# Second feed-forward of the last layer: opening weights one column sooner, seven opening tiles, kept first half, inputs of the way back made beside the last tile

## The chip, the cores and the metric

The kernel runs on one core of one Trainium2 chip. The metric is the device time of one execution in microseconds (us), as the median of several runs. The core has five engines that work through their own instruction lists in order: TensorE (PE, matrix products), VectorE (DVE), ScalarE (ACT), GpSimd (POOL) and SyncE (SP, which here issues nearly all transfers).

## The reference

A diffusion backbone with `DEPTH = 2` layers on a latent stream of 1024 positions of width 1024 and a context of 256 positions. All is float32. Each layer mixes tokens in three ways, projects, adds with a gate, and then runs a gated feed-forward. Only the end of the last layer matters for this change:

```
x = x + g1 * einsum('blm,md->bld', mix, w_out[l])
h = modulate(rms_norm(x, norm2_g[l]), sh2, sc2)
g, u = split(einsum('bld,df->blf', h, w_ffn_in[l]))      # 1024 -> 2 x 2816
x = x + g2 * einsum('blf,fd->bld', silu(g) * u, w_ffn_out[l])   # 2816 -> 1024
```

In the last layer the context is no longer needed, so this tail runs on the 1024 latent positions alone.

## The kernel before

Values are held transposed: features on the 128 partitions, positions along the row. The 1024 positions are two halves of 512 (0 and 1), the width is 8 groups of 128 features (`KD = 8`), the hidden width 22 tiles of 128 (`NF = 22`). Each float32 matrix product is made of matmuls of 128x128 by 128x512 on operands that are split into a rounded upper part `hi` and a rest `lo`: hi*hi + hi*lo + lo*hi, three matmuls for each group of 128 inputs. The split of weights or values costs a cast (the `hi`) and a subtraction (the `lo`); mostly ScalarE casts and VectorE subtracts.

The tail of the last layer has four stages, one behind the other on TensorE.

*The last out-projection* (`out_proj`, L1143): for each half, eight output columns `d`, each of 24 matmuls. For each column VectorE adds the gated product to `x` (a SCALAR_TENSOR_TENSOR), ScalarE squares it and VectorE sums the squares; the new `x` is stored to the memory `XD` (`park`), to be read again at the end. The weights come from a `Stream` (L1966): raw tiles of 128x1024 loaded by SP some columns ahead, cast by ScalarE, lower half by VectorE. In column `d == KD - 3` of the second half `soon()` is called, which starts the stream of the next stage.

*The opening* (`fast_open`, L1375; first loop of `ffn_fast`, L1379). The feed-forward's first product uses a scheme of Strassen's kind: with the two halves of positions and of inputs and the gate and up weights as a 2 by 2 block product, seven products of 12 matmuls serve instead of eight: A11·B11, S2·T2, S1·T1, A12·B21, S3·T3, A22·T4 and S4·B22, 84 matmuls for each of 22 hidden tiles. A11·B11 and A12·B21 need only the first half of the positions. So the first `FIRST = 6` tiles get these two products (24 matmuls a tile) while the second half is still being normed. Their results, `kept`, stay on chip. The weights of the opening are cast and negated by ScalarE, and the lower half is made by an accumulating DMA that POOL issues (`lo=("d",)`).

Meanwhile `fast_norm1` (L1315) norms the second half and makes the operands B22, T1 to T4 out of both halves, in four turns `k` of two feature groups each (`k` and `k + 4`). A turn has, among others, four scalings (`scaled`, L1341: `x` times a column factor times the row's `1/rms`), two for half 1 and two for half 0. Half 0's scalings were made once already, in `norm_h` (L554) for `fast_norm0`. The turns are a generator (`lane`) that is stepped between the products, so that its instructions lie between the evacuations of the opening on VectorE and ScalarE. Between them a clock model (`Clock`, with `due`) decides how many steps come in at `self.adv()`. `self.finish("norm1")` issues whatever is left of it.

*The main loop* (second loop of `ffn_fast`): 22 tiles of five or seven products. A generator `prep` casts and subtracts each operand of the weights up to `AHEAD = 7` products before it is used, in tiles from the pool `big` (23 buffers). The gated hidden values are stored to `HD` in memory: for each tile one store for each half of the positions.

*The way back* (`ffn_back`, L1539): for each half and each of 8 output columns, 66 matmuls (22 hidden tiles of three). Before its first column it reads half 0's 22 hidden tiles from `HD` (`fetch`), splits each one, 20 of them into the pool `part`, two into `big`, and loads `x` from `XD` and the weights `w_ffn_out` in three groups a column (8, 8 and 6 tiles). Half 1's tiles are fetched inside the last two columns of half 0.

Instructions are issued by a helper, so that most carry L166 (or L278 for matmuls) and are known by their tiles: `big`, `half` and `part` are pools of on-chip tiles, `bank` is PSUM, where the products land, `mod` and `db` are columns of factors, `rn` the row norms.

## Time and profile before

| | |
|---|---|
| median of 3 runs | 3127.68 us (3113.27 to 3129.17) |
| the profiled execution | 3125.03 us, its span 3123.2 us |
| TensorE busy | 2887.5 us, 92% of the span, 14308 matmuls |
| VectorE busy | 1917.5 us, 61% |
| ScalarE busy | 1174.0 us, 38% |
| GpSimd busy | 684.9 us, 22% |
| mean granted TensorE clock | 0.957 of 2.4 GHz |

In the views, `x12` behind a row is the number of like instructions that are shown as one; a bracket says how long the engine stood idle before and what ended it. A timeline has the start in us from the span's beginning, then the busy time of the group. A granted clock of 0.50 is 1.2 GHz and 1.00 is 2.4 GHz; a value between is a mix of both in that stretch.

### The profile page before, as it was taken

The numbers are of one execution on the slowest core, as the hardware profiler recorded it, in microseconds if no ns is written. First come the engines' busy times: TensorE is split into PE (matmuls) and PEld (weight loads), VectorE is DVE, ScalarE is ACT, GpSimd is POOL, SyncE is SP. The second block draws the span as 40 slices with busy tenths as digits, with TensorE's granted clock in tenths as the row PEclk, the third lists the DMA queues.
The fourth block names the chain that finished last, engine by engine and source line by source line (L and its number), as shares of the span: only waits on it lengthen the run. The fifth ranks groups of instructions, "written<-read, shape, count | busy, mean of one in ns | idle before, by whom it ended". The sixth has DMA issues, their size and how long they took to land.

```text
span 3123.2 us, 38190 instructions
## 1 busy us (share of the span) xinstructions
PE 2887.5 (92%) x14308; PEld 2375.1 (76%) x14308; DVE 1917.5 (61%) x2983; ACT 1174.0 (38%) x2021; POOL 684.9 (22%) x699
## 2 busy tenths in 40 slices
PE   7799878988799999999999889999988899996999
PEld 3687767866688888888888768878866688885887
DVE  5777778967845454444333488769935866665241
ACT  4554367733422222221222235457725322223131
POOL 0100047810223232232333000038800000000000
PEclk9899979999899999999999989999989899998999
DMA  6565642265222222221110225662255332224463
GB/s 217 139 152 137 203 133 77 89 231 202 93 80 69 75 81 81 73 81 44 41 37 32 95 69 123 170 208 71 79 172 145 108 98 81 81 68 145 126 204 94
DMA packets 205288, 351.70 MB, mean 113 GB/s; under 512 B 17072, under 2 KB 103728, under 8 KB 205104
## 3 DMA queue, kind: packets, MB, share of 16 engines
q1 hardware_dynamic: 197904, 327.24, 32.9%
q0 software_dynamic: 7200, 22.02, 4.1%
q8 instruction: 113, 1.85, 0.2%
q14 instruction: 71, 0.58, 0.1%
HBM read 284.18 MB, written 65.01 MB: 112 GB/s over the span
## 4 chain that ended last, share of the span: by engine, by line
PE 69%; DVE 14%; DMA 6%; ACT 5%; issue 5%; POOL 1%; SPq 0%; ACTq 0%; DVEq 0%; POOLq 0%
PE bank L278 64%; DVE st L166 4%; DVE half L166 4%; DVE big L166 3%; PE S L278 2%; DMA half<-in_w_mod 2%; PE bank L283 2%; DVE at L166 1%; ACT half L166 1%; ACT big L166 1%; ACT p L166 1%; POOL p L166 1%; DVE part L166 1%; DMA big<-XD 1%; DMA part<-in_w_mod 1%
## 5 line engine op out<-in xcount | busy, mean ns | idle before, releaser
L278 PE MATMUL bank<-part,big 128*128 128x512 f32 (+1 forms) x7656 | 1676.3, 376 | 104.6 <-ACT big L166 49.1
L278 PEld LDWEIGHTS bank<-part,big 128*128 128x128 f32 x7656 | 1345.1, 192 | 386.5 <-ACT big L166 52.7
L166 ACT CAST big<-big 128x1024 fp32r<-128x1024 f32 (+3 forms) x316 | 270.5, 866 | 193.1 <-DMA big<-in_w_ffn_out 139.0
L278 PE MATMUL bank<-half,big 128*128 128x512 f32 (+1 forms) x1584 | 325.9, 363 | 16.4 <-DVE big L166 7.2
L278 PEld LDWEIGHTS bank<-half,big 128*128 128x128 f32 x1584 | 264.6, 192 | 72.8 <-ACT half L166 13.7
L278 PE MATMUL bank<-big,big 128*128 128x512 f32 x1152 | 303.0, 402 | 6.0 <-ACT big L166 4.0
L166 DVE TENSOR_TENSOR big<-big,bank 128x512 f32<-128x512 f32 (+1 forms) x92 | 58.7, 677 | 401.8 <-PE bank L278 233.6
L166 DVE SCALAR_TENSOR_TENSOR big<-bank,mod,big 128x512 f32<-128x512 f32 (+1 forms) x384 | 266.2, 731 | 50.9 <-PE bank L278 33.2
L166 POOL TENSOR_TENSOR big<-big,big 128x1024 fp32r<-128x1024 f32 x71 | 175.3, 2480 | 454.6 <-ACT big L166 354.7
L166 DVE TENSOR_TENSOR big<-big,big 128x512 fp32r<-128x512 f32 (+6 forms) x243 | 212.6, 884 | 90.0 <-ACT big L166 88.3
L278 PEld LDWEIGHTS bank<-big,big 128*128 128x128 f32 x1152 | 220.3, 193 | 60.6 <-ACT big L166 5.3
L166 ACT ACTIVATE half<-bank,mod 128x256 f32<-128x256 f32 x160 | 75.9, 475 | 426.3 <-PE bank L278 406.0
L166 POOL TENSOR_TENSOR p<-p,p 128x512 f32<-128x512 f32 (+1 forms) x200 | 221.6, 1108 | 16.7
L166 DVE TENSOR_REDUCE st<-S 128x1 f32<-128x1280 f32 (+1 forms) x144 | 196.0, 1362 | 12.7 <-PE S L278 12.7
L166 POOL TENSOR_TENSOR big<-big,half 128x256 f32<-128x256 f32 x160 | 122.5, 765 | 352.2 <-ACT half L166 352.2
L166 ACT ACTIVATE p<-S,st 128x1280 f32<-128x1280 f32 (+1 forms) x144 | 177.7, 1234 | 45.8 <-DVE st L166 43.1
L166 POOL TENSOR_SCALAR p<-p,st 128x512 f32<-128x512 f32 (+1 forms) x200 | 123.6, 618 | 246.3 <-DVE st L166 189.4
L278 PE MATMUL S<-kv,big 128*128 128x512 f32 (+1 forms) x672 | 162.3, 379 | 9.0 <-ACT p L166 8.5
L166 DVE TENSOR_TENSOR half<-half,bank 128x512 f32<-128x512 f32 (+1 forms) x164 | 104.6, 649 | 104.5 <-PE bank L278 103.7
L166 ACT CAST big<-half 128x512 fp32r<-128x512 f32 (+1 forms) x129 | 75.4, 599 | 219.7 <-DVE half L166 169.4
L278 PEld LDWEIGHTS S<-kv,big 128*128 128x128 f32 x672 | 123.8, 197 | 36.8 <-ACT p L166 14.2
L166 DVE SCALAR_TENSOR_TENSOR big<-big,dww,big 128x1009 f32<-128x1009 f32 (+14 forms) x120 | 148.8, 1272 | 0.4
(123 smaller groups left out, 2759.3 us busy)
## 6 DMA issues: line engine op xcount, KB each, us to landing
big<-in_w_ffn_in SPq DMA_DIRECT2D x94, 512.0 KB, 3.5
big<-in_w_ffn_out SPq DMA_DIRECT2D x54, 512.0 KB, 6.0
big<-in_w_mod SPq DMA_DIRECT2D x48, 512.0 KB, 3.7
big<-in_w_out SPq DMA_DIRECT2D x40, 512.0 KB, 5.0
half<-in_w_mod SPq DMA_DIRECT2D x64, 256.0 KB, 5.6
big<-QS SPq DMA_DIRECT2D x128, 128.0 KB, 5.1
big<-in_w_in SPq DMA_DIRECT2D x28, 512.0 KB, 4.6
HD<-half SPq DMA_DIRECT2D x44, 256.0 KB, 2.0
```

Of the source, the lines that this page charges most:

```text
L166: r = fn(*a, **k)
L278: self.tc.nc.tensor.matmul(out, lhsT, rhs, start=start, stop=stop)
L283: self.tc.nc.tensor.transpose(out, in_, ident)
```

## The change

There are three parts.

*The opening.* `soon()` of the out-projections that park their output is called one column sooner (`KD - 4`), and the opening's stream then loads three raw tiles and splits two of them there (`ahead(3, 2)` for `ahead(2, 1)`). `FIRST` is 7: a seventh tile makes its A11·B11 and A12·B21 in the opening and not in the main loop. The first weights of the main loop (`load(2)`) are asked for ahead of `finish("norm1")`.

*The norm.* `norm_h` with `keep` writes the scaled values of half 0 over `x` (which is parked in `XD` already), and `fast_norm1` reads them there: eight SCALAR_TENSOR_TENSOR go. The mixed values of half 0 and the block `blk` are dropped earlier.

*The way back's inputs.* A generator `fast_end` is stepped at the last tile's products (its first step comes at tile 20). It reads half 0's hidden tiles 0 to 19 from `HD` two at a time (512 KB each) into `big`, splits them, and loads and splits the way back's first three weight groups. Tiles 20 and 21 of half 0 are split from the chip, and not stored. Each operand of the last products (`B11`, `T2`, ...) is dropped as soon as its last product is issued, so that its buffers come free. `ffn_back` gets the finished tiles and the weight stream.

```
-FIRST = 6
+FIRST = 7
...
-                t = self.half()[:, :w]
+                t = xs[k] if keep else self.half()[:, :w]
                 nc.vector.scalar_tensor_tensor(t, xs[k], a[:, k:k + 1], rs, ALU.mult, ALU.mult)
...
-                if soon is not None and b == n - 1 and d == KD - 3:
+                if soon is not None and b == n - 1 and d == KD - (4 if park is not None else 3):
                     soon()
...
-            t12 = scaled(k, 1, rs1)
-            t11 = scaled(k, 0, rs0)
-            nc.vector.tensor_tensor(t11, t12, t11, ALU.subtract)
+            t12, t11 = scaled(k), self.half()
+            nc.vector.tensor_tensor(t11, t12, xs[k][0], ALU.subtract)
...
-            t21 = scaled(m, 0, rs0)
-            nc.vector.scalar_tensor_tensor(t21, t21, b[:, m:m + 1], t11, ALU.add, ALU.subtract)
+            t21 = self.half()
+            nc.vector.scalar_tensor_tensor(t21, xs[m][0], b[:, m:m + 1], t11, ALU.add, ALU.subtract)
...
+        load(2)
+        self.finish("norm1")
...
+        hid, back = [{}, {}], []
+        end = self.fast_end(l, ops, hid, back)
         for f in range(NF):
             whole = f >= FIRST
+            step = lambda: next(end, None) if f == NF - 1 else None
+            if f == NF - 2:
+                next(end)
...
-            store.append((f, 0, u3))
+            if f < NF - 2:
+                store.append((f, 0, u3))
+            else:
+                hid[0][f] = self.pair()
+                self.split(*hid[0][f], u3)
...
+    def fast_end(self, l, ops, hid, back):
+
+        nc = self.nc
+        raws = []
+
+        def load(f):
+            t = self.big((2, 512))
+            nc.sync.dma_start(t, self.HD[f:f + 2, :, 0:512].rearrange("f p c -> p f c"))
+            raws.append((f, t))
+
+        def split(n):
+            for _ in range(n):
+                f, t = raws.pop(0)
+                for j in range(2):
+                    hid[0][f + j] = self.pair("part")
+                    self.split(*hid[0][f + j], t[:, j, :])
+
+        st = self.fast_out(l)
+        back.append(st)
+        st.load_to(1)
+        load(0)
+        load(2)
+        yield
+
+        del ops["B11"]
+        split(2)
+        load(4)
+        load(6)
+        yield
+
+        del ops["T2"]
+        st.split_to(1)
+        split(1)
+        load(8)
+        yield
+
+        del ops["T1"]
+        st.load_to(2)
+        split(1)
+        load(10)
+        yield
+
+        del ops["B21"]
+        split(2)
+        st.split_to(2)
+        st.load_to(3)
+        load(12)
+        yield
+
+        del ops["T3"]
+        split(1)
+        load(14)
+        yield
+
+        del ops["T4"]
+        split(1)
+        st.split_to(3)
+        load(16)
+        load(18)
+        yield
+
+        del ops["B22"]
+        split(2)
...
-        for f in range(NF):
-            fetch(0, f, "part" if f < 20 else None)
...
-                plan[0].ahead(2, 1)
+                plan[0].ahead(3, 2)
```

How this stands in the engines' lists is shown at three places. First ScalarE at the end of the last out-projection, from the cast of column 5's weights on (`part` with `mod` is half 0's norm, `half<-big` the square of a finished column). The list before:

```order
L166 CAST big_20013<-big_19913 128x1024
L166 ACTIVATE part_19819<-half_20042,mod_10680 128x512
L166 ACTIVATE half_20047<-big_19666 128x512
L166 CAST big_20051<-big_19967 128x1024
L166 CAST big_20057<-big_20055 128x1024
L166 ACTIVATE big_20058<-big_20057 128x1024
L166 ACTIVATE part_19820<-half_20086,mod_10680 128x512
L166 ACTIVATE half_20094<-big_19704 128x512
L166 CAST big_20098<-big_20011 128x1024
```

and of the changed kernel at the same place, where column 5's cast is `big_20008`:

```order
L166 CAST big_20008<-big_19913 128x1024
L166 CAST big_20014<-big_20012 128x1024
L166 ACTIVATE big_20015<-big_20014 128x1024
L166 CAST big_20021<-big_20019 128x1024
L166 ACTIVATE big_20022<-big_20021 128x1024
L166 ACTIVATE part_19819<-big_19704,mod_10680 128x512
L166 ACTIVATE half_20057<-big_19666 128x512
L166 CAST big_20061<-big_19964 128x1024
L166 ACTIVATE half_20091<-big_19704 128x512
L166 CAST big_20095<-big_20006 128x1024
```

`big_20014` and `big_20021` are tiles 0 and 1 of the opening, each a cast and a negation (ACTIVATE). Four such operations now stand between the casts of two neighbouring out-projection columns (`big_20008` and `big_20061`). Before, tile 0's two (`big_20057`, `big_20058`) stood behind the corresponding cast, `big_20051`.

Second, VectorE in the second turn of the second half's norm (`half<-big,mod,half` scales, `big<-big,bank` evacuates a product of the opening). Before:

```order
L166 SCALAR_TENSOR_TENSOR half_20347<-big_19535,mod_9879,half_20238 128x512
L166 SCALAR_TENSOR_TENSOR half_20349<-big_19535,mod_9879,half_19928 128x512
L166 TENSOR_TENSOR half_20349<-half_20347,half_20349 128x512
L166 TENSOR_TENSOR big_20279<-big_20279,bank_20343 128x512
L166 SCALAR_TENSOR_TENSOR half_20371<-big_19704,mod_9879,half_20238 128x512
L166 SCALAR_TENSOR_TENSOR half_20347<-half_20347,db_20240,half_20371 128x512
L166 TENSOR_TENSOR part_20353<-half_20349,part_20352 128x512
L166 SCALAR_TENSOR_TENSOR half_20349<-half_20371,mod_10680,half_20349 128x512
L166 SCALAR_TENSOR_TENSOR part_20374<-half_20371,mod_10680,part_20373 128x512
L166 TENSOR_TENSOR part_20378<-half_20347,part_20377 128x512
L166 SCALAR_TENSOR_TENSOR half_20407<-big_19704,mod_9879,half_19928 128x512
L166 SCALAR_TENSOR_TENSOR half_20407<-half_20407,mod_10680,half_20349 128x512
```

and now:

```order
L166 SCALAR_TENSOR_TENSOR half_20369<-big_19535,mod_9879,half_20257 128x512
L166 TENSOR_TENSOR half_20371<-half_20369,big_19535 128x512
L166 SCALAR_TENSOR_TENSOR half_20384<-big_19704,mod_9879,half_20257 128x512
L166 SCALAR_TENSOR_TENSOR half_20369<-half_20369,db_20259,half_20384 128x512
L166 TENSOR_TENSOR part_20374<-half_20371,part_20373 128x512
L166 TENSOR_TENSOR big_20307<-big_20307,bank_20377 128x512
L166 SCALAR_TENSOR_TENSOR half_20371<-half_20384,mod_10680,half_20371 128x512
L166 SCALAR_TENSOR_TENSOR part_20387<-half_20384,mod_10680,part_20386 128x512
L166 TENSOR_TENSOR part_20391<-half_20369,part_20390 128x512
L166 SCALAR_TENSOR_TENSOR half_20430<-big_19704,mod_10680,half_20371 128x512
L166 TENSOR_TENSOR part_20415<-half_20371,part_20414 128x512
```

The scalings of `big_19535` and `big_19704` by half 0's norm (`half_19928`) are gone; the subtraction and the sum read `big_19535` and `big_19704` themselves.

Third, SP's list at the end of the main loop, before:

```order
L166 DMA half_23565<-HD 128x512
L166 DMA half_23570<-HD 128x512
L166 DMA half_23575<-XD 128x512
L166 DMA big_23578<-in_w_ffn_out 128x8x128
L166 DMA big_23584<-in_w_ffn_out 128x8x128
L166 DMA big_23586<-in_w_ffn_out 128x6x128
L166 DMA big_23588<-in_w_ffn_out 128x8x128
L166 DMA big_23590<-in_w_ffn_out 128x8x128
L166 DMA big_23592<-in_w_ffn_out 128x6x128
```

and now:

```order
L166 DMA HD<-half_23199 128x512
L166 DMA big_23406<-in_w_ffn_out 128x8x128
L166 DMA big_23416<-HD 128x2x512
L166 DMA big_23453<-in_w_ffn_out 128x6x128
L166 DMA big_23455<-HD 128x2x512
L166 DMA big_23482<-HD 128x2x512
L166 DMA big_23514<-HD 128x2x512
L166 DMA big_23516<-HD 128x2x512
L166 DMA HD<-half_23361 128x512
L166 DMA half_23551<-XD 128x512
L166 DMA big_23554<-in_w_ffn_out 128x8x128
L166 DMA big_23556<-in_w_ffn_out 128x8x128
```

Before, the last of 22 reads from `HD` stand ahead of the first weights `w_ffn_out`, and all of them behind the last stores. Now the reads (`128x2x512`, two tiles each) and the first weight groups lie between the stores of tiles 20 and 21 (`HD<-half_23361` is the last store), and the load of `x` and the second column's weights behind it.

## Rows read from the trace of the kernel before

**Rows 1.** The page: the span, TensorE's busy time, share and instructions, and the shares of the engines in the chain of work that ended last.

```profile
span 3123.2 us, 38190 instructions
...
PE 2887.5 (92%) x14308; PEld 2375.1 (76%) x14308; DVE 1917.5 (61%) x2983; ACT 1174.0 (38%) x2021; POOL 684.9 (22%) x699
...
PE 69%; DVE 14%; DMA 6%; ACT 5%; issue 5%; POOL 1%; SPq 0%; ACTq 0%; DVEq 0%; POOLq 0%
```

**Rows 2.** What TensorE waited for: first in 2375 to 2465, then from 2440 to the end. The columns are the total in us, the number of waits and the longest.

```profile
PE bank L278 <- ACT big L166: 14.6, 1, 14.6
PE bank L278 <- DMA big<-in_w_ffn_in: 9.8, 2, 8.8
...
PE bank L278 <- ACT big L166: 39.4, 2, 24.8
```

**Rows 3.** Stretches of the span: length, busy us of each engine (instructions), the granted clock, the DMA share and rate.

```profile
2325.00:2330.00 5.00, 5.00 (x12) 3.88 (x13) 1.14 (x2) 1.05 (x2) 0.00 (x0) 0.50 0.41 158
...
2440.00:2460.00 20.00, 10.57 (x37) 8.40 (x38) 16.70 (x26) 7.33 (x12) 0.00 (x0) 0.65 0.14 53
...
2500.00:2600.00 100.00, 100.00 (x433) 81.03 (x432) 68.75 (x108) 27.41 (x48) 0.00 (x0) 1.00 0.30 95
...
2860.00:2870.00 10.00, 0.00 (x0) 0.00 (x0) 9.23 (x15) 7.90 (x14) 0.00 (x0) 0.50 1.08 370
2870.00:2880.00 10.00, 8.38 (x25) 6.25 (x26) 5.93 (x6) 5.85 (x6) 0.00 (x0) 0.65 1.17 310
```

**Rows 4.** TensorE's timeline at an earlier short wait.

```profile
2323.47 0.74 PE L278 MATMUL bank<-big,big 128*128 128x512 f32 x2 [2.24 <-ACT big L166]
2324.73 2.08 PE L278 MATMUL bank<-big,big 128*128 128x512 f32 x4 [0.52 <-DVE big L166]
2326.61 2.76 PE L278 MATMUL bank<-part,big 128*128 128x512 f32 x6
```

**Rows 5.** SP's timeline (the issue of transfers) at the end of the out-projection.

```profile
2366.18 0.38 SPq L166 DMA_DIRECT2D big<-in_w_out  x1
...
2371.03 0.87 SPq L166 DMA_DIRECT2D big<-in_w_ffn_in  x2
```

**Rows 6.** ScalarE's timeline at the end of the out-projection and in the opening. The row at 2371.16 casts the weights of column 6, the two behind it are tile 0 of the opening, and the one at 2406.43 copies the second half's scale.

```profile
2371.16 1.03 ACT L166 CAST big<-big 128x1024 fp32r<-128x1024 f32 x1
2375.25 1.05 ACT L166 CAST big<-big 128x1024 fp32r<-128x1024 f32 x1 [3.06 <-DMA big<-in_w_ffn_in]
2376.33 1.06 ACT L166 ACTIVATE big<-big 128x1024 fp32r<-128x1024 f32 x1
2377.29 0.71 ACT L166 ACTIVATE part<-half,mod 128x512 fp32r<-128x512 f32 x1
...
2378.43 1.03 ACT L166 CAST big<-big 128x1024 fp32r<-128x1024 f32 x1
...
2406.43 0.59 ACT L166 COPY half<-bank 128x512 f32<-128x512 f32 x1 [1.32 <-PE bank L283]
```

**Rows 7.** TensorE's timeline: the start of column 6 of the out-projection, and the three rows of the opening and of the first main product that have a wait ahead.

```profile
2374.20 2.98 PE L278 MATMUL bank<-part,big 128*128 128x512 f32 x12
...
2398.15 0.79 PE L278 MATMUL bank<-part,big 128*128 128x512 f32 x1 [8.75 <-DMA big<-in_w_ffn_in]
...
2421.04 13.75 PE L278 MATMUL bank<-part,big 128*128 128x512 f32 x58 [1.02 <-DMA big<-in_w_ffn_in]
2449.43 2.92 PE L278 MATMUL bank<-part,big 128*128 128x512 f32 x6 [14.64 <-ACT big L166]
```

**Rows 8.** VectorE's timeline: the first and the last scaling and subtraction of the second half's norm, and the first preparation for the main loop.

```profile
2407.05 1.41 DVE L166 SCALAR_TENSOR_TENSOR half<-big,mod,half 128x512 f32<-128x512 f32 x2 [5.51 <-ACT half L166]
...
2445.86 1.46 DVE L166 TENSOR_TENSOR big<-half,big 128x512 fp32r<-128x512 f32 x2
2447.24 0.68 DVE L166 TENSOR_TENSOR half<-big 128x512 f32<-128x512 f32 x1
```

**Rows 9.** TensorE's timeline at the end of the main loop and the start of the way back.

```profile
2845.92 0.86 PE L278 MATMUL bank<-big,big 128*128 128x512 f32 x3
2871.58 16.88 PE L278 MATMUL bank<-part,big 128*128 128x512 f32 x60 [24.80 <-ACT big L166]
```

**Rows 10.** ScalarE's and then VectorE's timeline of the same place: casts of the read-backs, the first weight cast; an evacuation of the loop, lower halves of the read-backs, lower halves of weights.

```profile
2852.50 0.62 ACT L166 CAST part<-half 128x512 fp32r<-128x512 f32 x1 [4.33 <-DMA half<-HD]
...
2856.72 7.37 ACT L166 CAST part<-half 128x512 fp32r<-128x512 f32 x11 [0.89 <-DMA half<-HD]
...
2870.48 1.04 ACT L166 CAST big<-big 128x1024 fp32r<-128x1024 f32 x1 [1.72 <-DMA big<-in_w_ffn_out]
...
2844.03 0.69 DVE L166 TENSOR_TENSOR half<-half,bank 128x512 f32<-128x512 f32 x1 [0.77 <-PE bank L278]
...
2857.37 7.44 DVE L166 TENSOR_TENSOR part<-half,part 128x512 fp32r<-128x512 f32 x11 [0.81 <-ACT part L166]
...
2890.56 2.35 DVE L166 TENSOR_TENSOR big<-big,big 128x1024 fp32r<-128x1024 f32 x2
```

**Rows 11.** Transfers issued in 2845 to 2885, with their number, size and the median us from issue to landing; and the landing times of all transfers to and from `HD` (shortest, median, longest).

```profile
half<-HD SPq DMA_DIRECT2D x22, 256.0 KB, 5.4
big<-in_w_ffn_out SPq DMA_DIRECT2D x6, 512.0 KB, 6.9
...
DMA to landing us min/median/max: 2.0/3.7/8.6
```

More of the change, by code (lines that the diff above doesn't have):

```diff
@@ L552, in sq_acc, with norm_h @@
             self.nc.vector.tensor_tensor(acc, acc, t, ALU.add)
-    def norm_h(self, xs, rs, a, b, blk):
+    def norm_h(self, xs, rs, a, b, blk, keep=False):
         nc = self.nc
@@ L1308, in fast_norm0 @@
     def fast_norm0(self, ops, xs, acc, l, blk):
-        ops["rs0"] = yield from self.rms(acc)
+        rs = yield from self.rms(acc)
         while not all((l, c) in self.M for c in (3, 4)):
             yield 1.5
-        yield from self.norm_h([x[0] for x in xs], ops["rs0"], self.M[l, 4][:, 0, :], self.M[l, 3][:, 0, :], blk)
+        yield from self.norm_h([x[0] for x in xs], rs, self.M[l, 4][:, 0, :], self.M[l, 3][:, 0, :], blk, True)
     def fast_norm1(self, ops, xs, acc, l):
@@ L1319, in fast_norm1 @@
         rs1 = yield from self.rms(acc)
-        rs0 = ops["rs0"]
         a, b = self.M[l, 4][:, 0, :], self.M[l, 3][:, 0, :]
@@ L1339, in op, with scaled @@
                 return ops[n][k]
-            def scaled(kk, e, rs):
+            def scaled(kk):
                 t = self.half()
-                nc.vector.scalar_tensor_tensor(t, xs[kk][e], a[:, kk:kk + 1], rs, ALU.mult, ALU.mult)
+                nc.vector.scalar_tensor_tensor(t, xs[kk][1], a[:, kk:kk + 1], rs1, ALU.mult, ALU.mult)
                 return t
-            t12 = scaled(k, 1, rs1)
-            t11 = scaled(k, 0, rs0)
-            nc.vector.tensor_tensor(t11, t12, t11, ALU.subtract)
+            t12, t11 = scaled(k), self.half()
+            nc.vector.tensor_tensor(t11, t12, xs[k][0], ALU.subtract)
             T1 = op("T1")
@@ L1351, in fast_norm1 @@
             yield "v"
-            t22 = scaled(m, 1, rs1)
+            t22 = scaled(m)
             B22 = op("B22")
@@ L1384, in ffn_fast @@
         ops["B21"] = [(blk.hi[k], blk.lo[k]) for k in range(H, KD)]
+        del blk
         def prod(w, n):
@@ L1440, in pair @@
                 ready.append((f, n, (hi, lo)))
-            load(2)
             for f in range(NF):
@@ L1500, in ffn_fast @@
                 nc.scalar.copy(p1, prod(take(f, "A11"), "B11"))
+                step()
             else:
@@ L1504, in ffn_fast @@
             vec(u2, p1, prod(take(f, "S2"), "T2"), ALU.subtract)
+            step()
             p5 = prod(take(f, "S1"), "T1")
             stores()
+            step()
             if whole:
@@ L1509, in ffn_fast @@
                 self.act(s, s, AF.Silu)
+                step()
             del p1
@@ L1515, in ffn_fast @@
             del p5
+            step()
             vec(u3, u3, prod(take(f, "A22"), "T4"), ALU.add)
             vec(u3, s, u3, ALU.mult)
-            store.append((f, 0, u3))
+            if f < NF - 2:
[3 more added lines that the diff above has]
+                self.split(*hid[0][f], u3)
             del s, u3
+            step()
             vec(u2, u2, prod(take(f, "S4"), "B22"), ALU.add)
@@ L1524, in ffn_fast @@
             del u2, c22
+            step()
             if f == NF - 1:
-                ops.clear()
                 stores()
+        return hid, back[0]
+    def fast_end(self, l, ops, hid, back):
[50 more added lines that the diff above has]
+        split(2)
     def fast_out(self, l):
@@ L1537, in fast_out, with ffn_back @@
         return Stream(self, aps, raw_ahead=2, split_ahead=3)
-    def ffn_back(self, l, st, gate, final):
+    def ffn_back(self, l, st, hid, gate, final):
         nc = self.nc
-        hid = [{}, {}]
         def fetch(b, f, where):
@@ L1811, in mixed @@
                     self.finish("sub")
+                    loc[0] = None
+                    for k in range(4):
+                        del self.mix[k, 0]
                 for k in range(4):
@@ L1888, in run @@
                 xt.clear()
-                self.ffn_fast(l, plan.pop(), ops, h2.pop())
-                self.ffn_back(l, self.fast_out(l), self.mod(l, 5, 0), final)
+                hid, back = self.ffn_fast(l, plan.pop(), ops, h2.pop())
+                self.ffn_back(l, back, hid, self.mod(l, 5, 0), final)
                 ph.close()
```

1 line of the change is left out of this document (removed).

## The prediction

> **What bounds the kernel now.** I read the page first. TensorE is busy for 2887.5 us of a span of 3123.2 and holds 69% of the chain that ended last [rows 1]: it bounds the kernel, and its idle time or slow clock is what a change can win. I then asked for the waits of TensorE from the last out-projection to the end. The reader is to see a few long waits and nothing else: 14.6 us on ScalarE and 9.8 us on the feed-forward weights' DMAs between 2375 and 2465, and 39.4 us on ScalarE after 2440, of which 24.8 is one wait [rows 2] (the other is the 14.6). Between the two ends TensorE never idles: in 2500:2600 it is busy for all 100 us, 433 matmuls, 0.231 us each, at full clock [rows 3]. So the change can touch two places: the opening (stage A) and the handover to the way back (stage B).
>
> Then the clock, by windows. Behind each gap it is low: 0.65 in 2440:2460, 0.65 in 2870:2880 against 1.00 in 2500:2600 [rows 3], which are mixes of 1.2 and 2.4 GHz. In 2870:2880 25 matmuls took 8.38 us where 25 x 0.231 = 5.8 are needed, 2.6 us lost. A gap as short as 2.24 us does this too: at 2323.47 TensorE had waited 2.24 us, then 0.52 more, and the next twelve matmuls took 0.74, 2.08 and 2.76 us [rows 4], with 2325:2330 at a clock of 0.50 [rows 3]; 5.58 us instead of 2.77 is 2.8 us lost on top of 2.8 us idle.
>
> **Stage A, the opening.** Before, tile 0's weights are issued by SP at 2371.03 [rows 5] and cast at 2375.25, 4.2 us later [rows 6]; tile 1's lower half is late, TensorE waits 8.75 us at 2398.15, 1.02 at 2421.04 and 14.64 at 2449.43 [rows 7].
>
> Step 1, weights one column sooner. SP now issues three raw tiles behind the out-projection's load at 2366.18 [rows 5], the first at about 2366.6, instead of after that column's store. That costs no transfer, but ScalarE is in order, and its row shows cast and negate of tiles 0 and 1 *ahead* of the cast of the out-projection's weights for column 6. Before, that cast is at 2371.16 [rows 6] and column 6 begins at 2374.20 [rows 7]. After: raw 0 lands 4.2 us after its issue, 2370.8; four operations at 1.08 and 0.96 us from start to start [rows 6] end at 2374.9; a square and one norm operation, some 1.2; the cast 1.03; so about 2377.2, and DVE's lower half 1.2 behind it (two took 2.35 us, [rows 10]). Column 6 then waits 3.0 us and again 0.5, and drops to 1.2 GHz for about 2.9 us as at 2323: **6.5 us lost**, new. Bounds from the quickest and the slowest landing of another 256 KB transfer of this stage, 2.0 and 8.6 us [rows 11]: with 2.0 the cast is 0.8 late, and I count 1; with 8.6 all of it is 4.4 more, 11.
>
> By the Trainium skill, page "TensorE: Matmul & The Clock Gate", section "Part 1: The HAM clock gate", the count of slow matmuls behind an idle stretch is not fixed, but differs between runs of one kernel. It gives 6, 11 or 14; at 0.22 us lost on each that is an estimate of 1.3 to 3.1 us where I put 2.9. The rows at 2323 and 2872 lie at its upper end. By the page the sum could be 1.6 us better at each restart.
>
> Step 2, the 8.75 and 1.02 us. Tiles 0 and 1 are ready long before the last column ends, and SP's next raw tiles have no store ahead of them but those of the last columns. Both waits go: 9.8 us and the half-clock stretch behind the first, some 3 us. But that moves only matmuls ahead of norm 1; what decides is when norm 1 ends.
>
> Step 3, norm 1. VectorE starts it at 2407.05, when ScalarE's copy of the second half's scale is done [rows 6], and works almost without a pause until 2447.24, 40.2 us; then 2.2 us of preparing the first main operand until TensorE starts at 2449.43 [rows 7, 8]. Its start hardly moves: the opening begins 6.5 us later, its wait of 8.75 is gone, and the copy now stands behind one more tile's split on ScalarE, 2406.5 to 2407. Kept first halves remove 8 scalings (two in each of four turns): 8 x 0.70 (two took 1.41 us, [rows 8]) is 5.6 us. One more evacuation add, 0.6, comes in: 2407 + 40.2 - 5.6 + 0.6 + 2.2 = 2444.4. There is a second path: the seventh tile's add sits ahead of the last turn, and it has to wait for the end of the opening, 2392.5 + 7 x 24 x 0.231 + 1.5 for sums and transposes = 2433. Then the add, 11 operations at 0.68 (7.5) and the 2.2 give 2443.4. The later counts: TensorE starts at 2444.4 instead of 2449.4, **5.0 us**.
>
> Step 4, the seventh opening tile. 24 of its matmuls are done before 2433 instead of after 2449: 24 x 0.231 = **5.5 us** less in the main loop.
>
> The new loss of step 1 is inside the 2392.5, so A gives 5.0 + 5.5 = 10.5 us. Bounds: 16 with a stall of 1 us at column 6 (everything 5.5 sooner, the scale's copy too); 6 with that stall 4.4 us longer. Since raw 0's landing of 4.2 us is from the same transfer in the same place, I take 10.5.
>
> **Stage B, the handover.** TensorE's last matmul of the loop ends at 2846.78, the way back starts at 2871.58 [rows 9]. In between 22 read-backs of 256 KB are issued and split one after the other, ScalarE's first at 2852.50, and the way back's weights are behind them, cast at 2870.48 [rows 10]. With 2.6 us of clock behind it the place costs 24.8 + 2.6 = 27.4 us.
>
> After, the read-backs are ten of 512 KB, spread over the last two tiles, with the three weight groups among them: 5.24 + 1.44 = 6.7 MB. The windows show 370 GB/s in this traffic [rows 3], 18 us; a tile is 84 matmuls, 19.4 us, and the loads begin a tile earlier. Each landing took 5.4 us for 256 KB in the crowded stretch [rows 11]. What they need is room in the `big` pool, which each finished operand of the loop gives back; by the order each waits for a product of tile 20 or 21, none for a split of the one before. The Trainium skill, "DMA: Bandwidth & Descriptors", section "Specifications", gives about 358 GB/s for one core's HBM share; the trace has 370 and decides. By the page the estimate is 18.7 us and changes nothing.
>
> VectorE's part: in the last tile 20 lower halves (11 took 7.44 us, 0.68 each, [rows 10]), 13.5 us; three weight groups, 3.4; eleven evacuations at 0.69 [rows 10], 7.6: 24.5 us against 19.4 of TensorE. It runs on some 5 to 8 us into the first column of the way back. That column needs a tile's pair every 3 matmuls, 0.69 us, in the order in which they are split, so the last ones are needed 14 us after it starts: hidden. ScalarE has 20 casts at 0.67 [rows 10], 2.9 for the weights and some 6 of the loop's, 22 us, the same. The second column's weights are issued behind the last store, near 2849, land 6.9 us later [rows 11], and are cast and split by 2859.5; needed at 2846.8 + 66 x 0.231 = 2862. Two to three us of slack. I take 1.4 us for what is left of the gap: **26 us** gained. Bounds: 27.4, and 18 if the second column is late by 5 us and restarts slowly (5 + 2.8), with 1.6 at the gap itself.
>
> Tiles 20 and 21 of the first half never go through HBM: 2 of 44 stores and 2 read-backs less, hidden either way. Freeing two names early and the third read-ahead cost nothing that a wait shows.
>
> **Sum.** 10.5 + 26 = 36.5 us: 3125.03 - 36.5 = 3088.5 for the profiled execution; it lies 2.65 below the median of three, whose spread is 15.9. I predict 3089.
>
> **The rivals.**
> 1. *Hardly a stall at column 6, both places close.* Raw 0 lands as quickly as the quickest store. For: column 6's weights were 2 us early before. Against: the order puts 4.1 us of work and a landing ahead of them. Time: 3125.0 - 16 - 27.4 = 3082, down to 3074 without any wait there and with both slow restarts of the opening gone (3 us each).
> 2. *The way back stumbles.* VectorE's 24.5 us push the evacuations of the last tile, or the second column's weights are late: 8 us, 3097. For: the slack is 2 to 3 us. Against: the needs come in the order of the work.
> 3. *The opening gives nothing*: the stall at column 6 is twice as long and norm 1 still waits for the seventh tile, which would come at 2440: 3099 to 3108.
> 4. *Slower*: the read-backs wait for room. If `big` slots are only freed when the previous pair is split, each of ten goes alone, 5.4 landing + 2.5 of four casts and lower halves = 7.9 us, 79 in all; less one tile as cover, 19.4, the gap is 60 instead of 24.8, 35 us more, and with A's 10.5 the time is 3150. It decides the sign where the gap passes 24.8 + 10.5 = 35.3 us, with 79 / (35.3 + 19.4) = 1.4 loads in flight or fewer. For: 23 slots, all used by the loop. Against: the order's waits named above.
> 5. *Nothing happens*: the copies land no earlier, 3125.
>
> **How the numbers follow.** Forecast (3082 to 3094) 0.52; rival 1 0.16; rival 2 0.13; rival 3 0.10; rival 4 0.05; rival 5 0.04. I call no change what is within 0.5%, 15.6 us, about what a measurement here can tell: 3112 to 3143. Faster: the first four, 0.91, less 0.03 that the spread of runs may carry over 3112, 0.88; same 0.08; slower 0.04. Range: from rival 1's lower end to just short of rival 3's upper, 3074 to 3107.
>
> **What would show it.** Right: a wait of 2 to 4 us on ScalarE at column 6 of the last out-projection, with a clock of 0.50 behind it; no wait on the feed-forward weights' DMA; norm 1 five us shorter; a wait of 10 to 11 us on ScalarE before the first main product; the gap at the handover under 3 us, with the clock at 1.00 through it, VectorE filled through the last tile and some us beyond. Wrong: no wait at column 6 (step 1), a main product at the same distance from the copy of the scale (step 3), a wait on DMA or VectorE over 4 us in the first two columns of the way back (stage B).

## The result and the profile after

The changed kernel takes 3087.15 us (median of four runs, 3085.5 to 3088.5) against 3122.72 us before (four runs, 3113.3 to 3129.2). The ratio is 0.9888, its 95% interval 0.9858 to 0.9919: 35.6 us, or 25 to 44, are won. The prediction was 3089 us. The profiled execution has a span of 3086.7 us, 36.5 less than before.

What TensorE waited for in the profiled execution after, from the last out-projection to the first products of the main loop (total us, times, longest):

```profile
PE bank L278 <- ACT big L166: 14.9, 3, 10.7
PE bank L278 <- DMA big<-in_w_ffn_in: 2.1, 1, 2.1
PE bank L278 <- DVE big L166: 0.5, 1, 0.5
```

The 24.8 us at the handover of [rows 2] is in no list any more, the 14.6 has become 10.7, the 9.8 on DMAs 2.1, and a new wait on ScalarE has come in. Its place is in TensorE's timeline, which answers to [rows 7]:

```profile
2369.46 2.93 PE L278 MATMUL bank<-big,big 128*128 128x512 f32 x12
2376.25 5.69 PE L278 MATMUL bank<-part,big 128*128 128x512 f32 x12 [3.86 <-ACT big L166]
2381.78 2.95 PE L278 MATMUL bank<-big,big 128*128 128x512 f32 x12
...
2402.09 2.08 PE L278 MATMUL bank<-part,big 128*128 128x512 f32 x4 [2.05 <-DMA big<-in_w_ffn_in]
2403.96 1.05 PE L283 MATMUL bank<-ident,rn 128*128 128x128 f32 x4
2404.66 29.82 PE L278 MATMUL bank<-part,big 128*128 128x512 f32 x126
2445.21 2.93 PE L278 MATMUL bank<-part,big 128*128 128x512 f32 x6 [10.72 <-ACT big L166]
```

The row at 2376.25 is column 6 of the out-projection. Twelve matmuls take 5.69 us behind the wait, where 2.96 is the rule. ScalarE's timeline of the same time (it answers to [rows 6]) shows what it waits for:

```profile
2364.34 1.03 ACT L166 CAST big<-big 128x1024 fp32r<-128x1024 f32 x1
2369.97 1.05 ACT L166 CAST big<-big 128x1024 fp32r<-128x1024 f32 x1 [4.59 <-DMA big<-in_w_ffn_in]
2371.05 1.06 ACT L166 ACTIVATE big<-big 128x1024 fp32r<-128x1024 f32 x1
2372.02 1.03 ACT L166 CAST big<-big 128x1024 fp32r<-128x1024 f32 x1
2373.08 1.06 ACT L166 ACTIVATE big<-big 128x1024 fp32r<-128x1024 f32 x1
2374.04 0.70 ACT L166 ACTIVATE part<-big,mod 128x512 fp32r<-128x512 f32 x1
2374.65 0.61 ACT L166 ACTIVATE half<-big 128x512 f32<-128x512 f32 x1
2375.17 1.03 ACT L166 CAST big<-big 128x1024 fp32r<-128x1024 f32 x1
```

ScalarE stands idle for 4.59 us for the opening's raw tile 0, works through its cast and negation and those of tile 1 (1.05 each), one operation of half 0's norm and a square, and only then casts column 6's weights, at 2375.17.

VectorE's norm of the second half after (rows of [rows 8]): its first scaling, the adds of the fifth and of the seventh opening tile, and the first preparation for the main loop.

```profile
2405.67 0.75 DVE L166 SCALAR_TENSOR_TENSOR half<-big,mod,half 128x512 f32<-128x512 f32 x1 [5.31 <-ACT half L166]
...
2426.13 0.69 DVE L166 TENSOR_TENSOR big<-big,bank 128x512 f32<-128x512 f32 x1 [0.89 <-PE bank L278]
...
2434.87 0.68 DVE L166 TENSOR_TENSOR big<-big,bank 128x512 f32<-128x512 f32 x1
...
2443.05 0.68 DVE L166 TENSOR_TENSOR half<-big 128x512 f32<-128x512 f32 x1
```

It takes 37.4 us (2443.05 - 2405.67) where it took 40.2. At 2426.13 VectorE waits 0.89 us for the fifth tile's product; from there to the end of the norm it has no further wait over 0.15 us. The handover, TensorE after (it answers to [rows 9]):

```profile
2836.28 0.86 PE L278 MATMUL bank<-big,big 128*128 128x512 f32 x3
2836.98 13.95 PE L278 MATMUL bank<-part,big 128*128 128x512 f32 x60
2850.77 1.54 PE L278 MATMUL bank<-big,big 128*128 128x512 f32 x6
2852.33 0.73 PE L278 MATMUL bank<-part,big 128*128 128x512 f32 x2
2853.59 13.65 PE L278 MATMUL bank<-part,big 128*128 128x512 f32 x58 [0.53 <-DVE big L166]
```

The way back starts without a gap, and its second column waits 0.53 us. SP asks for that column's weights only behind the last store, 9.7 us after the way back has begun:

```profile
2846.72 5.41 SPq L166 DMA_DIRECT2D big<-in_w_ffn_out  x5
```

The stretches of the last tile and of the first column (columns as in [rows 3]):

```profile
2817.00:2837.00 20.00, 20.00 (x88) 16.18 (x88) 16.47 (x25) 12.46 (x22) 0.00 (x0) 1.00 0.78 262
2837.00:2857.00 20.00, 19.45 (x84) 15.27 (x83) 13.95 (x21) 9.09 (x13) 0.00 (x0) 1.00 0.52 152
```

VectorE is busy for 16.5 of 20 us, the clock is at 1.00 in both. The ten read-backs landed as follows (to be read beside [rows 11]):

```profile
big<-HD SPq DMA_DIRECT2D x10, 512.0 KB, 4.6
```

### The profile page after: what moved, and what is told of

Same layout as the page of the kernel before. It is cut to its first block, busy times and chain, and to the rows that moved or that the text cites. A ratio compares the mean times of both kernels' runs of the same rounds, so it can differ in the third digit from the quotient of the medians.

```text
span 3086.7 us, 38151 instructions
## 1 busy us (share of the span) xinstructions
PE 2881.6 (93%) x14308; PEld 2370.2 (77%) x14308; DVE 1910.0 (62%) x2973; ACT 1173.7 (38%) x2021; POOL 686.4 (22%) x700
## 4 chain that ended last, share of the span: by engine, by line
PE 70%; DVE 14%; DMA 5%; ACT 5%; issue 5%; POOL 1%; SPq 0%; ACTq 0%; DVEq 0%; POOLq 0%
PE bank L278 65%; DVE st L166 4%; DVE big L166 3%; DVE half L166 3%; PE S L278 2%; PE bank L283 2%; DVE at L166 2%; DMA half<-in_w_mod 2%; ACT p L166 1%; ACT big L166 1%; ACT half L166 1%; DVE part L166 1%; DVE rn L166 1%; DMA part<-in_w_mod 1%; ACT at L166 1%
## 5 line engine op out<-in xcount | busy, mean ns | idle before, releaser
L166 ACT CAST big<-half 128x512 fp32r<-128x512 f32 (+1 forms) x129 | 75.5, 599 | 221.1 <-DVE half L166 164.7
L278 PEld LDWEIGHTS S<-kv,big 128*128 128x128 f32 x672 | 124.8, 198 | 38.6 <-ACT p L166 15.7
```

The costliest lines, as they stand in the source:

```text
L166: r = fn(*a, **k)
L278: self.tc.nc.tensor.matmul(out, lhsT, rhs, start=start, stop=stop)
```

## The experiments

The stages lie one behind the other on TensorE, and what stands ahead of them takes between 2360 and 2374 us in these executions, with the same instructions. So each run is read from one place on: the start of column 5 of the last out-projection, at 2368.62 before, 2366.66 after. "Norm" is VectorE's time from the first scaling with the second half's scale to the first preparation for the main loop. All but the time are worked out from the timelines of the profiled executions. The time is the median of four runs for before, changed, e4, e5, e6 and e11, and a single run for the others, which are read by their stages alone.

| kernel | time us | norm starts | norm takes | first main product | from it to the end | column 5 to the end |
|---|---|---|---|---|---|---|
| before | 3122.7 | 38.4 | 40.2 | 80.8 | 673.8 | 754.6 |
| changed | 3087.2 | 39.0 | 37.4 | 78.6 | 641.5 | 720.0 |
| e1 back only | 3092.0 | 38.6 | 40.4 | 81.1 | 647.5 | 728.7 |
| e2 late open | 3095.6 | 37.7 | 38.6 | 78.5 | 641.8 | 720.4 |
| e3 six | 3087.1 | 37.9 | 35.4 | 75.5 | 648.1 | 723.5 |
| e4 split late | 3079.9 | 30.1 | 37.1 | 69.4 | 642.6 | 711.9 |
| e5 split late, eight | 3077.0 | 30.0 | 40.0 | 72.2 | 635.0 | 707.2 |
| e6 pool low | 3081.2 | 30.1 | 37.1 | 70.2 | 641.7 | 711.9 |
| e7 no keep | 3082.1 | 35.9 | 41.0 | 79.0 | 641.5 | 720.5 |
| e8 one slot | 3115.3 | 36.6 | 37.1 | 75.9 | 666.0 | 741.9 |
| e9 one by one | 3113.1 | 36.2 | 37.1 | 75.4 | 672.0 | 747.4 |
| e10 late lead | 3085.9 | 36.4 | 37.1 | 75.7 | 642.4 | 718.2 |
| e11 early scale, eight | 3077.5 | 27.2 | 43.1 | 72.4 | 636.0 | 708.4 |

The first product comes 2.2 us behind the norm's end in each (e6: 3.1). e8 to e10 have the changed kernel's opening unaltered, so the changed opening was executed four times: 78.6, 75.9, 75.4 and 75.7.

**e1: the way back's part alone.** The opening and the norm are put back:

```
-FIRST = 7
+FIRST = 6
...
-                if soon is not None and b == n - 1 and d == KD - (4 if park is not None else 3):
+                if soon is not None and b == n - 1 and d == KD - 3:
...
-                plan[0].ahead(3, 2)
+                plan[0].ahead(2, 1)
```

and `fast_norm0`, `fast_norm1` and `load(2)` are as before; `fast_end` stays.

> Only the way back's part of the change (inputs beside the last tile); opening and norm as before, six opening tiles. Theory, stages in series: from the start of column 5 of the last out-projection to the first product of the main loop 80.8 us as before, main loop 397.4 as before, no gap at the handover, way back 250: the time is 26.9 us below that of before, about 3096. Rival, the two halves of the change need each other (room in the big pool is only there because tiles 0 to 6 are done early): a gap of 5 us or more stays at the handover, over 3101.

Measured: 81.1 to the first product, no gap at the handover, and from the first product to the end 647.5 against 673.8: 26.3 us. The theory's 26.9 holds within 0.6, and the part doesn't need the other. The time of 3092 lies under the expected 3096 because what stands ahead of column 5 took 2361.5 us in this execution.

**e2: the opening's weights one column later again.** `KD - 3` and `ahead(2, 1)` in the changed kernel.

> The changed kernel with the opening's weights asked for one column later again (and two raw tiles, one split). Theory, the wait at column 6 is worth its price: no wait at column 6 (3.86 us and 2.7 of slow clock less), but the wait of about 8.8 us on tile 1 is back, the opening ends 4 us later, and the first main product comes 82 us after the start of column 5 instead of 78.6; time about 3091. Rival, the earlier weights give nothing and only cost the wait: 75 to 78 us, 3084 to 3087.

Measured: no wait at column 6, and the wait on tile 1 is back:

```profile
2403.43 0.79 PE L278 MATMUL bank<-part,big 128*128 128x512 f32 x1 [9.24 <-DMA big<-in_w_ffn_in]
...
2451.96 2.93 PE L278 MATMUL bank<-part,big 128*128 128x512 f32 x6 [8.11 <-ACT big L166]
```

The first product comes at 78.5, under the 82 of the theory and no later than in the changed kernel's own profile. The opening ends 2.6 us later than in the changed kernel's profile, not 4, and the first product follows its end by 8.1 us, where the changed kernel has 10.7: nine operations of VectorE start here between the last tile's add and the first product, 14 there. With eight tiles (e5, e11) it is 8.0, with nine operations as well. By this run alone the earlier weights give nothing. Beside the other three executions of the changed opening (75.4 to 75.9) they give 2.6 to 3.1 us. Which of the two is the usual price, one execution of e2 can't settle.

**e3: six opening tiles** in the changed kernel (`FIRST = 6`).

> The changed kernel with six opening tiles. Theory, VectorE's norm and not the end of the opening sets when the main loop starts: 77.9 us from column 5 to the first main product (one add of 0.6 less) and the main loop 5.5 longer, time about 3092. Rival, the seventh tile holds up the last turn of the norm, as the prediction had it for its second path: 73 to 74 us, main loop 5.5 longer, time about 3087.

Measured: 75.5, between the two. The norm takes 35.4, 1.6 to 2.0 less than with seven tiles, and from the first product to the end it is 6.6 longer. So the seventh tile costs the norm an add and a little waiting, some 2 us where the theory had 0.6, for 6 won in the loop. The first product itself comes no sooner than in three of the four executions with seven tiles; column 6 waits longer here, 4.51 us. Nor does the norm's own list alone set the start, as the theory had it: VectorE waits 1.39 us in it for the fourth tile's product, and from there to the norm's end for nothing over 0.15.

**e4: load early, split late.** The three raw tiles are still asked for at column 4, but each split stands behind the cast of the out-projection's next weights:

```
-                if soon is not None and b == n - 1 and d == KD - (4 if park is not None else 3):
-                    soon()
+                if soon is not None and b == n - 1:
+                    if park is None:
+                        if d == KD - 3:
+                            soon()
+                    elif d >= KD - 4:
+                        soon(d - (KD - 4))
...
-            def fast_soon():
-                plan.append(self.fast_open(l))
-                plan[0].ahead(3, 2)
+            def fast_soon(i):
+                if i == 0:
+                    plan.append(self.fast_open(l))
+                    plan[0].load_to(3)
+                elif i < 3:
+                    plan[0].split_to(i)
```

> The changed kernel with the three raw tiles of the opening still loaded at column 4, but tile 0 cast and negated at column 5 and tile 1 at column 6, behind the casts of the out-projection's own weights. Theory, the wait at column 6 is ScalarE's order alone, and all that follows moves with it: no wait at column 6, 72 us from column 5 to the first main product instead of 78.6, time about 3080.5. Rival, the start of the norm hangs on something else (the third raw tile, the copy of the scale behind the table load): 75 us or more, 3084 to 3087.

Measured: ratio to before 0.9862 (0.9844 to 0.9879), 3079.9 us.

```profile
2372.14 2.96 PE L278 MATMUL bank<-part,big 128*128 128x512 f32 x12
...
2394.35 1.20 PE L278 MATMUL bank<-part,big 128*128 128x512 f32 x4 [1.23 <-DMA big<-in_w_ffn_in]
...
2435.93 2.93 PE L278 MATMUL bank<-part,big 128*128 128x512 f32 x6 [10.79 <-ACT big L166]
```

Column 6 starts without a wait at full clock, and the first product comes at 69.4 (2.6 under the expected 72), 9.2 sooner than in the changed kernel's profile and 6.0 to 6.5 sooner than in its other three executions. The wait at column 6 was ScalarE's order alone. The four runs lie under all four of the changed kernel (3077.2 to 3081.6 against 3085.5 to 3088.5); the intervals of the two ratios overlap.

**e5: an eighth opening tile** on top of e4 (`FIRST = 8`).

> The kernel with the late split, and an eighth opening tile. Theory, there are 10.8 us of idle TensorE before the main loop, so 24 more matmuls fit: the opening ends 5.5 us later, the last add stands inside the last turn of the norm with six operations behind it, first main product 70 to 71.5 us after the start of column 5 (69.4 with seven), main loop 386.4 instead of 392.0; 4 us better than with seven, about 3076. Rival, the eighth tile holds two more buffers and the kept pair, and the main loop's first weights come late: 75 us or more, no gain.

Measured: 72.2 (0.7 over the expected range) and 635.0 to the end, 4.7 us better than e4 in the stages; 3077.0 us, ratio 0.9853 (0.9837 to 0.987). The intervals of e4 and e5 overlap, so between these two only the stages tell. No wait on the main loop's weights came up.

**e6: part of the norm on GpSimd** on top of e4:

```
-            low(t12, T3)
+            low(t12, T3, nc.gpsimd)
...
-            low(t21, T4)
+            low(t21, T4, nc.gpsimd)
```

> The kernel with the late split, and the lower halves of T3 and T4 (8 of 16 such subtractions in the second half's norm) on GpSimd instead of VectorE. Theory, VectorE's list in the norm sets the start of the main loop: 8 x 0.67 = 5.4 us less of it, first main product 64 to 65 us after the start of column 5 instead of 69.4, time about 3075. Rival, GpSimd is slower (1.1 us for 128x512 elsewhere in this kernel) and works on the same memory: VectorE's operations get longer beside it, or the seventh tile's accumulating DMA is late behind them, 69 us or more.

Measured: 70.2, nothing won; the norm takes 37.1 as in e4, with eight operations fewer on VectorE, and the four runs take 3070.3 to 3090.1 us. GpSimd's and VectorE's rows show why:

```profile
2406.54 2.86 POOL L166 TENSOR_TENSOR part<-half,part 128x512 fp32r<-128x512 f32 x2
...
2432.21 1.28 POOL L166 TENSOR_TENSOR big<-half,big 128x512 fp32r<-128x512 f32 x1 [3.33 <-ACT big L166]
```

```profile
2406.23 3.73 DVE L166 TENSOR_TENSOR part<-half,part 128x512 fp32r<-128x512 f32 x1 [1.26 <-ACT part L166]
...
2415.01 1.82 DVE L166 SCALAR_TENSOR_TENSOR half<-half,mod,half 128x512 f32<-128x512 f32 x1
...
2432.00 0.68 DVE L166 TENSOR_TENSOR big<-big,bank 128x512 f32<-128x512 f32 x1
2432.60 1.44 DVE L166 SCALAR_TENSOR_TENSOR half<-half,mod,half 128x512 f32<-128x512 f32 x1
```

An operation of 0.69 us takes 3.73 where GpSimd does two in 2.86, one of 0.75 takes 1.82. Five more are 0.7 to 1.0 longer, the one at 2432.60 among them. So VectorE gives away 5.4 us and loses some 8 by standing still (3.04 + 1.07 + five others, the last of them just behind the norm), of which shorter waits for other engines give part back. The rival holds, though its 1.1 us is low: GpSimd's operations on two tiles of 128x512 elsewhere in this kernel take 1.31 us in the mean. Even without the standing still the theory's 5.4 us were hardly to be had: in e4 VectorE already waits 1.8 us in the norm for the opening's products.

**e7: the kept scalings made again** in the changed kernel.

> The changed kernel with half 0's eight scalings made again in the norm of the second half. Theory, VectorE's list is nearly full and most of the eight (5.6 us) comes back, less what now lies in its short waits for products: 81 to 82 us from column 5 to the first main product instead of 78.6, main loop and way back the same. Rival, the seventh tile's end decides, and they are hidden: 78.6 to 80.

Measured: 79.0, which looks like the rival. But the norm takes 41.0, 3.6 to 3.9 more than with the kept values; it only started 3.1 us sooner than in the profile it is held against (35.9 against 39.0, the others 36.2 to 36.6). So the theory holds for the norm, and the comparison of the first product with one execution misleads: beside the other three it comes 3.2 to 3.6 later. Of 5.6 us of scalings some 1.8 lay in VectorE's short waits. But the rival has a part in it: VectorE waits 0.80 and 0.18 us for the products of the sixth and the seventh tile, the second time to the end of the opening, and has 20 operations from the seventh tile's add to the first product where the changed kernel has 14.

**e8: one buffer for the read-backs.**

```
-            t = self.big((2, 512))
+            t = one
```

with `one` allocated once. Read-backs are issued here ahead of the split of the one before, so most of the hidden tiles of half 0 hold a later pair's values. This kernel is read for its time alone.

> The changed kernel with all ten read-backs of the hidden tiles through one and the same buffer, so that each waits for the split of the one before. Theory (the fourth rival's price), what the way back's part wins is read-backs in flight: nine more loads of some 4.6 us landing and 2.5 of splitting after the first product of tile 21, 64 us, against 34 until they are needed last: 25 to 35 us back, as waits of 3 to 6 us each in the first column of the way back, time 3112 to 3122. Rival, the order of issue alone does it, and the read-backs fit one by one: 3087 to 3092.

Measured: from the first product to the end 666.0 against 641.5, 24.5 back. Since several loads are issued ahead of the split that they were to wait for, it is not the rival's case in full; e9 is.

**e9: one by one.** The same buffer, each load issued behind the split of the one before.

> The changed kernel with the read-backs of the hidden tiles through one buffer, each issued behind the split of the one before, nothing overwritten. Theory (the fourth rival's price, now in full), what the way back's part wins is read-backs in flight: each pair costs 4.6 us of landing and some 2.9 of splitting, 7.5, and ten of them from the first product of tile 21 on end 70 us later, with the last pair needed 33 us after that product: 33 to 38 us back, the same number of instructions, time about 3122. Rival, room and flight matter little and the order of issue does it: 3087 to 3095.

Measured: 672.0, 30.5 us back, a little under the 33 expected. TensorE in the first column of the way back:

```profile
2841.80 3.23 PE L278 MATMUL bank<-part,big 128*128 128x512 f32 x6 [4.66 <-ACT part L166]
2847.61 3.23 PE L278 MATMUL bank<-part,big 128*128 128x512 f32 x6 [2.58 <-ACT part L166]
2853.44 3.23 PE L278 MATMUL bank<-part,big 128*128 128x512 f32 x6 [2.61 <-ACT part L166]
2860.40 3.23 PE L278 MATMUL bank<-part,big 128*128 128x512 f32 x6 [3.74 <-ACT part L166]
2866.17 3.23 PE L278 MATMUL bank<-part,big 128*128 128x512 f32 x6 [2.54 <-ACT part L166]
2872.58 3.22 PE L278 MATMUL bank<-part,big 128*128 128x512 f32 x6 [3.18 <-ACT part L166]
```

Six pairs are waited for, 19.3 us, and each time six matmuls run at the slow clock, 3.23 where 1.56 is the rule, 10.0 us more. The rows lie 5.8 to 7.0 us apart. The part's whole gain is gone: it rests on read-backs in flight together.

**e10: the lead of one tile away**; the first two read-backs and the first weights start with tile 21 instead of 20.

```
-            if f == NF - 2:
+            if f == NF - 1:
```

> The changed kernel with the first two read-backs and the first weights of the way back asked for at the start of tile 21 instead of tile 20. Theory, the lead of one tile is spare but for the first landing (4.6 us, needed after 2.8): the first splits come 2 to 3 us late and the slack of the first column takes most of it; handover gap 0 to 3 us, 720 to 723 us from the start of column 5 to the end (720.0 in the changed kernel). Rival, all ten read-backs move by a tile's share of the queue and the first column waits several times: 727 or more.

Measured: no gap at the handover, 0.75 + 0.53 at the second column, 642.4 to the end against 641.5. The lead is spare: with it, e2 and e4 wait 1.2 us at the second column too.

**e11: the scale sooner**, on top of e5: the lag of 1.5 us with which the transposes of the second half's scale are planned is 0.

```
-        rs1 = yield from self.rms(acc)
+        rs1 = yield from self.rms(acc, LAG1)
```

> The kernel with the late split and eight tiles, and the second half's scale transposed as soon as it is there (its planned lag of 1.5 us set to 0), so that its copy stands ahead of tile 4's split on ScalarE. Theory, the norm's start sets the main loop's start: norm 2 us sooner, first main product 70 us after the start of column 5 instead of 72.2, time about 3075. Rival, tile 4's and later weights are late behind it and the opening waits: 72 us or more, nothing won.

Measured: the norm starts at 27.2, 2.8 sooner than in e5, and takes 43.1, 3.1 longer; the first product comes at 72.4. The rival holds, though by its end and not by its cause: the opening's waits on DMA are 0.88 and 0.25, but its end is where it was (64.4; 64.1 in e5), and with eight tiles the first product follows the opening's end by 8.0 in both. A sooner norm only waits more: VectorE's waits in it grow from 5.5 to 8.1 us.

## Why the prediction was right

**The sum.** 36.5 us were predicted for the profiled execution and 36.5 measured between the spans. That is closer than the reasoning deserves: 2.0 of it lie ahead of column 5, where nothing was changed. From column 5 on the profile shows 34.6 (754.6 - 720.0); with the changed opening's other three executions, 75.4 to 75.9 for 78.6, it would be 37 to 38.

**Stage B** was predicted with 26 and gave 26.8: the wait of 24.80, 1.9 in the rest of the way back (2.6 of slow clock expected there), and a wait of 0.53 at the second column, counted in. e1 confirms it alone. VectorE did run on, to 2848.2, 11 us into the first column, where 5 to 8 were said. The two to three us of slack for the second column's weights were not there. Their load stands behind the last store, and that store behind VectorE's run-on, so SP issues it 9.7 us after the way back has begun and not 2; it lands in 4.5 us instead of 6.9, and the column waits 0.53 us in the profile, up to 1.3 in e10.

The fourth rival was priced too high. It had a gap of 60 us, 35 more than before, and a time of 3150. In e9, with each read-back alone, the cost over no gap at all is 30.5 us and the time 3113.1, which is no loss against before (3121.7 in the same series): a pair takes 6.2 us in the mean of e9's rows and not 7.9, and the first column needs the pairs one by one, so most of their time is hidden. That the rival would not come about was argued from the waits in the order, and the profile shows it.

**Stage A, step 1.** The wait at column 6 was predicted as 3.0 + 0.5 with 2.9 of slow clock, 6.5; the profile has 3.86 and 2.73 (5.69 - 2.96), 6.6. The two parts differ a little: raw 0 landed 5.2 us after its issue and not 4.2, and the slow clock costs 1.8 to 3.1 us in the other executions with this order. The bounds, 2.0 and 8.6 us, were read from 256 KB transfers of the hidden tiles, another stage; raw 0 has 512 KB. e4 shows cause and price.

**Step 2** was wrong in one point: "both waits go". The wait of 8.75 went, but the opening waits 2.05 us on tile 2's lower half, 1.1 to 2.1 in every execution with this early start. The third raw tile lands early, but it is cast and negated only behind the last column's square, at 2391.65 in the profile, and its accumulating DMA comes behind that.

**Step 3** had two errors that cancel, so its number is in part luck. The norm was to get 5.0 shorter (40.2 to 35.2) and got 2.8 to 3.1 shorter: VectorE now waits 3.1 to 3.4 us in it for products and casts, against 0.9 before. Work taken from a full engine comes back in part as waiting for its neighbours. The norm's start was to stay; it came 1.8 to 2.2 sooner in three executions and 0.6 later in the profiled one. So the first product came 5 us sooner in three (80.8 to 75.4 - 75.9), as forecast, and 2.3 in the profiled one.

The path is another than said, too. Before, VectorE's list does run from the scale's copy to the end of the norm with no waits but two for casts, 0.9 us. After, it waits 0.30 and twice 0.89 us for the opening, the last time at 2426.13 for the fifth tile's product, and then runs through. TensorE had worked on the opening without a pause since 2402.09, when the lower half of its third tile (tile 2) had landed. So the opening's pace, and behind the fifth tile VectorE's list, set the start of the main loop. In the four executions of this opening the first product follows the opening's end by 10.72 or 10.73 us, the norm's start by 39.2 to 39.5. The second path was of this kind, with 10.4 us, but by the seventh tile's add; that add comes 0.4 us behind the opening's end without a wait. With eight tiles it is the same: in e5 the last wait, 0.89 us, is for the seventh tile's product, and e11 shows that a sooner norm wins nothing there. With seven tiles it is read from the trace; no run moves the norm's start alone.

**Step 4**: 5.5 predicted; the loop is 5.6 shorter (397.35 to 391.77).

Two of the signs did not come: a wait on the feed-forward weights' DMA is left (2.05 us), and the norm is not five us shorter. Of the rivals, the first (hardly a stall at column 6) was given 3082; it did not come about, but e4 takes the stall away by another order and measures 3080. The second and third did not come about.

## What to carry to other kernels

Ask for a transfer early, but put the work on it behind what the same in-order engine owes to the present stage: loading and splitting one column sooner cost 6 us that loading sooner alone did not. Work taken from an engine wins for certain only behind the last wait that the engine still has; ahead of it, it can come back as waiting. When a gap is filled by work beside the last tile, the number of transfers in flight decides; look whether each load waits for a product or for the one before. And before a stage's gain is read from two profiles, read the same stage in a few executions: here one opening differed by 3 us with the same instructions, and the part ahead of it by 14.

## What was not expected of the hardware

The granted clock doesn't fall behind each wait of the same length. Before, waits of 2.24 and 0.52 us were followed by ten matmuls and some more at the slow clock [rows 4] (the first two took 0.74 us in both executions); after, the same two waits in the same place were not:

```profile
2321.14 0.74 PE L278 MATMUL bank<-big,big 128*128 128x512 f32 x2 [2.24 <-ACT big L166]
2322.40 1.20 PE L278 MATMUL bank<-big,big 128*128 128x512 f32 x4 [0.52 <-DVE big L166]
2323.43 1.56 PE L278 MATMUL bank<-part,big 128*128 128x512 f32 x6
```

Likewise the opening's wait: 2.05 us in the changed kernel's profile, with four matmuls in 2.08 behind it, and 2.08 us in e10, with four in 1.20:

```profile
2400.10 1.20 PE L278 MATMUL bank<-part,big 128*128 128x512 f32 x4 [2.08 <-DMA big<-in_w_ffn_in]
```

The Trainium skill, "TensorE: Matmul & The Clock Gate", section "Part 1: The HAM clock gate", says that the count of slow matmuls at the start of a kernel varies from run to run, 6, 11 or 14; the prediction took this for restarts behind a wait. These rows agree that the count varies, behind a short wait too, and here it can be none. The slow clock makes up most of the 2.8 us between the opening of the profile and that of e10: 0.8 us behind the wait at column 6 and 1.6 behind the opening's.

VectorE stands still beside GpSimd: in e6 an operation on two on-chip operands took 3.73 us for 0.69 while GpSimd did two, but the add of a product in PSUM, at 2432.00, kept its 0.68 with GpSimd at work from 2432.21 on. The Trainium skill, "SBUF — State Buffer", section "SBUF: two separate sides", has this as an exclusive lock, taken for the whole instruction, between GpSimd and a VectorE operation with two inputs in SBUF. The trace agrees in the seven places where VectorE's operations got longer.
